# Gated branches summed in PSUM, rotary and router operands kept in PSUM, and the attention sink as one more score of each row

## The chip, the cores and the metric

One core of a Trainium2 chip runs the whole kernel as one program. The metric is the device time of one execution in microseconds (us); before the change it is 1878.28 us, the median of 3 runs (1877.82 to 1882.6). Engines are named as the profile names them: PE (TensorE), DVE (VectorE), ACT (ScalarE), POOL (GpSimd), SP (the queue that issues most DMAs).

## What is computed

One decoder layer, all in float32, for 512 prompt tokens and 8 sequences of 8 new tokens, model width 1024:

```python
z = x @ w_in                      # b_gate, c_gate, h_in, q, k, v, g_conv, g_attn
q, k = rotary(q), rotary(k)       # x * cos + swapped halves of x * (+-sin)
conv_y = short_conv(c_gate * h_in)                 # 3 taps
m = max(max(s), sink); p = exp(s - m)              # window of 128 keys, 8 query heads, 2 KV heads
attn_y = p / (sum(p) + exp(sink - m)) @ v
merged = sigmoid(g_conv) * ((b_gate * conv_y) @ w_conv_out) + sigmoid(g_attn) * (attn_y @ w_attn_out)
h = layer_norm(ALPHA * x + merged @ w_o)
# channel mixer: 8 heads, each the best 16 of 128 x 128 experts by two half keys
y = layer_norm(ALPHA * h + sum_j gate_j * gelu(h . u_j) * v_j)
```

## The kernel before, in words

The 576 tokens are worked in two groups. The first (chunks 0 and SMP: 128 prompt tokens, 64 new tokens and 64 more prompt tokens, 256 columns) has its experts gathered row by row; the second (chunks 1, 2 and 3, 320 tokens) is multiplied with all experts densely. A matmul in float32 is made of three, on a high and a low half of each operand: `split` (L118 to L120) writes the high half on ACT and the low half, the difference, on DVE or POOL. Every weight table of 128x1024 is split so on its way in (`table`, from L136): ACT makes the high half, and POOL or DVE, by the table's number, the low half. POOL's instructions are these subtractions, 2.4 us each for a table, and the issue of the gathers (L511).

Each group passes through these steps: `project_q` and `project_kv` (PSUM banks of pool "mm", of which there are 3), the rotary in `qkv_rope` (from L203), `attention` by chunk and KV head, `conv` by channel tile, `merge_conv`, `merge_attention` (8 tiles dt of 128 model channels, then w_o and the first layer norm), and `scores` with `route`.

In `qkv_rope`, DVE multiplies q and k, which lie in PSUM, by cosine into an SBUF tile t1 (L213) and by sine, with halves swapped, into t2 (L215), and adds the two (L219 for q, L223 for k). In `softmax_parts` (L245 to L265), called once for each chunk and KV head (10 times) and once for the new tokens, DVE takes each row's maximum (L252), its maximum with the sink (L253), the negation (L255) and the sink's difference (L257); ACT takes that one's exponential (L258) and those of the four heads' scores (L261), each with its sum; DVE adds the sink's share (L262). PE then transposes the weights (L301, L345), and DVE and ACT copy them to SBUF (L304, L306).

In `merge_attention`, for each dt PE makes the gate's product (24 matmuls) and the branch's (12 matmuls, in a bank of "mm"). ACT takes the sigmoid `sg` (L671), DVE multiplies it by the branch's product in PSUM (L674), adds the convolution's gated branch `br` (L675), and the sum is split (ACT L119, DVE L120, tiles mhi and mlo). In the PSUM pool "mm" a bank is free for the next product as soon as L674 has read it.

In `route` (L421 to L472), for 4 heads of one chunk at a time, DVE adds the candidates (L429, L432), takes the best 16 (L413 to L417), has ACT take exponentials (L446, L447), normalises (L449 to L451), and finds by integer arithmetic on 64 columns in two passes (L462 to L467) and a comparison with a row of numbers (L469 to L472) which keys they were. From the second group's routing on, that row of numbers lies in columns 384 to 512 of a PSUM tile, `shared[0]`, whose other columns `gate_matrix` (L772 on) fills later with transposes. `route` is called 4 times for the first group and 5 times for the second.

Beside all this runs side work, `experts` (L490): gathers by POOL of rows of the expert tables, one row for each token of the first group at a time, and one DVE instruction of 1024 columns for each (L525, L534). They are put in after weight tables by fixed paces (`side`).

The order of the instructions on each engine is laid out for the whole program by the framework's planner, which follows the data's dependences on a simulated timeline (`TileContext(..., schedule_with_timeline_sim=True)`); the program's order is its priority. On each engine the instructions then run in that fixed order. `late` and `in_order` add orders by hand, on the DMA queue of SP and on PE, and none of them is on a line that changes.

## Time and profile before

| | |
|---|---|
| Median of 3 runs | 1878.28 us |
| The profiled execution | 1882.06 us, its span 1880.3 us |
| PE busy | 1733.5 us (92%) |
| DVE busy | 1507.2 us (80%) |
| POOL busy | 1111.2 us (59%) |
| ACT busy | 782.1 us (42%) |
| Mean granted clock of PE | 0.964 |

Busy time is that in which an engine works on an instruction; for DVE and POOL that includes time in which the instruction has begun and stands. An engine's idle time is put down to the work of another engine that it waited for. The timeline's times are from the start of the span. [...]

### The profile page before, as it was taken

To read this page: it belongs to the slowest core of one execution; us is meant where nothing else is said; L and a number is where in the kernel's file an instruction comes from. 1 tells how busy PE (TensorE), PEld (TensorE's weight loads), DVE (VectorE), ACT (ScalarE), POOL (GpSimd) and SP (SyncE) were. 2 spreads that over 40 slices of the span, in tenths; PEclk is the share of its full clock that TensorE was granted. 3 is DMA by queue.
4 is the path that set the end of the run, shared out by engine and by line. 5 is a ranking of instruction groups with operands and counts; after the bars stand their busy time and mean duration, and the time that the engine had idled before them with its cause. 6 is when DMAs were issued, how large, how long until landed. Compare 5 with 4: busy or idle time off the path is not lost.

```text
span 1880.3 us, 27617 instructions
## 1 busy us (share of the span) xinstructions
PE 1733.5 (92%) x9760; PEld 1573.5 (84%) x9760; DVE 1507.2 (80%) x2632; ACT 782.1 (42%) x1339; POOL 1111.2 (59%) x724
## 2 busy tenths in 40 slices
PE   7999998897989998699979899999999999999985
PEld 7997798887779888699978777787899999998974
DVE  6646689998955699998896677878778888888897
ACT  4554343442333433367785333333333333343322
POOL 4445433466756667688835522223578777778883
PEclk9999999997989999799999899999999999999998
DMA  7445443357757678799947999999989999989973
GB/s 246 156 134 213 130 135 118 113 186 254 277 192 249 232 239 276 248 326 363 338 187 253 330 327 328 345 336 341 322 311 353 335 327 353 350 299 339 326 264 108
DMA packets 190539, 496.50 MB, mean 264 GB/s; under 512 B 17712, under 2 KB 83696, under 8 KB 187312
## 3 DMA queue, kind: packets, MB, share of 16 engines
q1 hardware_dynamic: 135104, 293.39, 45.5%
q0 software_dynamic: 55296, 201.35, 30.1%
q8 instruction: 76, 1.25, 0.3%
q14 instruction: 63, 0.52, 0.1%
HBM read 454.48 MB, written 40.54 MB: 263 GB/s over the span
## 4 chain that ended last, share of the span: by engine, by line
PE 49%; DVE 24%; DMA 10%; issue 7%; POOL 5%; ACT 5%; SPq 1%; DVEq 0%; POOLq 0%; ACTq 0%
PE acc L937 19%; PE ps L123 9%; PE ps L124 8%; PE ps L125 8%; POOL wlo L120 3%; DMA re<-spill 3%; DVE junk L525 3%; PE ps L794 2%; POOL g L511 2%; DVE wlo L120 2%; DMA raw<-in_euT 2%; ACT whi L119 1%; ACT hot L791 1%; DMA g<-in_eu,idx 1%; DVE s L415 1%
## 5 line engine op out<-in xcount | busy, mean ns | idle before, releaser
L120 POOL TENSOR_TENSOR wlo<-raw,whi 128x1024 fp32r<-128x1024 f32 x232 | 580.0, 2503 | 320.6 <-ACT whi L119 287.9
L119 ACT ACTIVATE whi<-raw 128x1024 fp32r<-128x1024 f32 x388 | 409.2, 1056 | 590.0 <-PE ps L124 235.9
L123 PE MATMUL ps<-xhi,whi 128*128 128x384 f32 (+2 forms) x1600 | 531.3, 332 | 34.3 <-ACT sp L860 27.8
L125 PE MATMUL ps<-xhi,wlo 128*128 128x384 f32 (+2 forms) x1600 | 527.4, 330 | 1.6 <-POOL wlo L120 1.6
L124 PE MATMUL ps<-xlo,whi 128*128 128x384 f32 (+2 forms) x1600 | 527.6, 330 | 0.0
L534 DVE SCALAR_TENSOR_TENSOR h<-g,pre,h 128x1024 f32<-128x1024 f32 x192 | 316.2, 1647 | 71.7 <-DMA g<-in_ev,idx 70.4
L511 POOL DMA_INDIRECT g<-in_eu,idx x192 | 206.6, 1076 | 241.3 <-DVE junk L525 186.5
L123 PEld LDWEIGHTS ps<-xhi,whi 128*128 128x128 f32 x1600 | 309.6, 194 | 44.3 <-ACT sp L860 30.3
L511 POOL DMA_INDIRECT g<-in_ev,idx x192 | 255.0, 1328 | 126.5 <-DVE h L534 87.3
L124 PEld LDWEIGHTS ps<-xlo,whi 128*128 128x128 f32 x1600 | 309.3, 193 | 3.6 <-issue 0.9
L125 PEld LDWEIGHTS ps<-xhi,wlo 128*128 128x128 f32 x1600 | 308.6, 193 | 3.0 <-POOL wlo L120 2.1
L937 PE MATMUL acc<-whi,chi 128*128 128x512 f32 x756 | 292.4, 393 | 14.7 <-ACT chi L119 8.4
L937 PE MATMUL acc<-wlo,chi 128*128 128x512 f32 x756 | 299.6, 396 | 5.7 <-POOL wlo L120 5.7
L937 PE MATMUL acc<-whi,clo 128*128 128x512 f32 x756 | 258.1, 394 | 2.1 <-DVE clo L120 2.1
L120 DVE TENSOR_TENSOR wlo<-raw,whi 128x1024 fp32r<-128x1024 f32 x156 | 204.6, 1312 | 49.1 <-ACT whi L119 48.9
L937 PEld LDWEIGHTS acc<-whi,chi 128*128 128x128 f32 x756 | 143.1, 189 | 47.1 <-ACT chi L119 11.7
L937 PEld LDWEIGHTS acc<-wlo,chi 128*128 128x128 f32 x756 | 144.1, 191 | 37.0 <-POOL wlo L120 8.2
L525 DVE SCALAR_TENSOR_TENSOR junk<-g,hp 128x1024 bf16<-128x1024 f32 x104 | 125.7, 1209 | 56.9 <-DMA g<-in_eu,idx 54.8
L937 PEld LDWEIGHTS acc<-whi,clo 128*128 128x128 f32 x756 | 143.6, 190 | 32.8 <-DVE clo L120 2.7
L785 DVE TENSOR_TENSOR hot<-pt,T 128x1024 f32<-128x1024 f32 x96 | 114.0, 1217 | 17.1 <-PE ps L794 12.1
L525 DVE SCALAR_TENSOR_TENSOR junk<-g,h 128x1024 bf16<-128x1024 f32 x88 | 123.7, 1406 | 3.1 <-DMA g<-in_eu,idx 2.8
L794 PE MATMUL ps<-hot 128*128 128x128 f32 x768 | 111.6, 289 | 15.2 <-ACT hot L791 14.0
(252 smaller groups left out, 2205.5 us busy)
## 6 DMA issues: line engine op xcount, KB each, us to landing
raw<-in_euT SPq DMA_DIRECT2D x128, 512.0 KB, 6.1
raw<-in_ev SPq DMA_DIRECT2D x128, 512.0 KB, 5.0
gd<-gb SPq DMA_DIRECT2D x24, 1024.0 KB, 5.2
gm<-gd SPq DMA_DIRECT2D x48, 512.0 KB, 9.7
raw<-in_w_g SPq DMA_DIRECT2D x32, 512.0 KB, 3.4
raw<-in_w_pq SPq DMA_DIRECT2D x32, 512.0 KB, 4.2
raw<-in_w_bch SPq DMA_DIRECT2D x24, 512.0 KB, 3.5
spill<-sp SPq DMA_DIRECT2D x60, 192.0 KB, 4.2
```

The lines of the kernel that those rows point to most:

```text
L119: A.activation(hi, src, AF.Copy)
L120: return (eng or V).tensor_tensor(lo, src, hi.bitcast(F32), op=ALU.subtract)
L123: PE.matmul(ps, L[0], R[0], start=start, stop=False)
L124: PE.matmul(ps, L[0], R[1], start=False, stop=False)
L125: PE.matmul(ps, L[1], R[0], start=False, stop=stop)
L415: V.match_replace(s2, val[:, 0:8], s, -3.0e38)
L511: G.indirect_dma_start(out=rows[i], out_offset=None, in_=I[src], in_offset=bass.IndirectOffsetOnAxis(ap=idx[c][:, s:s + 1], axis=0))
L525: V.scalar_tensor_tensor(junk, g, 1.0, in_psum(c), op0=ALU.mult, op1=ALU.mult, accum_out=p)
L534: V.scalar_tensor_tensor(h_tok[c], g, p, h_tok[c], op0=ALU.mult, op1=ALU.add)
L785: V.tensor_tensor(hot, iota_ps.unsqueeze(1).unsqueeze(1).broadcast_to([128, 2, 4, 128]), T[:, 0:2, n:n + 4].unsqueeze(3).broadcast_to([128 ...
L794: newest[1] = PE.matmul(ps[:, r * 128:(r + 1) * 128], hot[:, 1, r, :], oi, start=True, stop=True).ins
L937: PE.matmul(*args, **kw)
```

## The change

It changes four places.

- `qkv_rope`: the product with cosine is written in place, into the projection's PSUM bank, after the two products with sine have read it; the adds (L219, L223) then read one operand from PSUM.
- `softmax_parts`: the score tile gets one more column for each row and head, into which ACT copies the sink. The row maximum is taken over all columns and written negated in one instruction, the exponentials run over all columns, and their sum holds the sink's share. The maximum with the sink, the negation, the difference, its exponential and the final addition go. Both callers make the tile one column wider; the sink's weight is in a column that no transpose reads.
- `route`: the tiles mk, u1 and gs lie in columns 0 to 132 of `shared[0]` in PSUM, once that tile is there, which is for the second group.
- `merge_attention`: the product with `sg` and the sum with `br` are written in place into the product's PSUM bank, and the split reads it from there.

```diff
--- before.py
+++ after.py
@@ -208,12 +208,12 @@
         out = {}
         for nm, ps, nh in (("q", pq, 8), ("k", pkv, 2)):
             src = ps[:r, :nh * 64].rearrange("p (h d) -> p h d", d=64)
-            t1 = tmp("t", [128, 8, 64], "qT", "r1", 2)[:r, :nh]
+            t1 = src
             t2 = tmp("t", [128, 8, 64], "o", "r2", 2)[:r, :nh]
-            V.tensor_tensor(t1, src, cos.broadcast_to([r, nh, 64]), op=ALU.mult)
             for a, b in ((0, 32), (32, 0)):
                 V.tensor_tensor(t2[:, :, a:a + 32], src[:, :, b:b + 32],
                                 sin[:, a:a + 32].unsqueeze(1).broadcast_to([r, nh, 32]), op=ALU.mult)
+            V.tensor_tensor(t1, src, cos.broadcast_to([r, nh, 64]), op=ALU.mult)
             x = tmp("t", [128, nh * 64], nm + "r", bufs=3)[:r]
             if nm == "q":
                 V.tensor_tensor(x.rearrange("p (g k d) -> p k g d", g=4, k=2),
@@ -243,23 +243,18 @@
         return pt.rearrange("p (g n) -> p g n", g=4)[:, :, :r], pk[:, :r]
 
     def softmax_parts(s, sink, name):
-        r, n = s.shape[:2]
+
+        r, n, m = s.shape
 
         def small(tag):
             return tmp("t", [128, n], tag, name + tag, 2)[:r]
 
-        mx = small("mx")
-        V.tensor_reduce(mx, s, axis=AX.X, op=ALU.max)
-        V.tensor_tensor(mx, mx, sink, op=ALU.max)
+        A.activation(s[:, :, m - 1:m], sink.unsqueeze(2), AF.Copy)
         ngm = small("ngm")
-        V.tensor_scalar(ngm, mx, -1.0, None, op0=ALU.mult)
-        es = small("es")
-        V.tensor_tensor(es, sink, mx, op=ALU.subtract)
-        A.activation(es, es, AF.Exp)
+        V.tensor_reduce(ngm, s, axis=AX.X, op=ALU.max, negate=True)
         den = small("den")
         for i in range(n):
             A.activation(s[:, i, :], s[:, i, :], AF.Exp, bias=ngm[:, i:i + 1], accum_out=den[:, i:i + 1])
-        V.tensor_tensor(den, den, es, op=ALU.add)
         rd = small("rd")
         V.reciprocal(rd, den)
         return rd
@@ -284,7 +279,8 @@
         mask = mask_p[:r, k0 + 128 - q0:k0 + 128 - q0 + nk]
         o = tmp("t", [128, 4, 2, 64], "o", bufs=2)[:r]
         for kv in range(2):
-            st = tmp("t", [128, 1024], "t4", bufs=3)[:r].rearrange("p (g k) -> p g k", g=4)[:, :, :nk]
+            sa = tmp("t", [128, 1028], "t4", bufs=3)[:r].rearrange("p (g k) -> p g k", g=4)[:, :, :nk + 1]
+            st = sa[:, :, :nk]
             for gp2 in range(2):
                 ps = bank("at")[:r]
                 for j in range(2):
@@ -293,7 +289,7 @@
                 V.scalar_tensor_tensor(st[:, gp2 * 2:gp2 * 2 + 2, :],
                                        ps.rearrange("p (j k) -> p j k", j=2)[:, :, :nk], SCALE,
                                        mask.unsqueeze(1).broadcast_to([r, 2, nk]), op0=ALU.mult, op1=ALU.add)
-            rd = softmax_parts(st, sink_p[:r, kv * 4:kv * 4 + 4], "p")
+            rd = softmax_parts(sa, sink_p[:r, kv * 4:kv * 4 + 4], "p")
             pT = tmp("t", [128, 1024], "t4", bufs=3).rearrange("p (b g n) -> p b g n", b=2, g=4)[:, :, :, :r]
             for b, (at, n, _, _) in enumerate(blocks):
                 ps = bank("at")
@@ -324,7 +320,8 @@
         qf = qT.rearrange("p b g t -> p (b g t)")
         mask_s = tmp("t", [128, 2, 192], "mask_s")
         late(mask_s, I["mask_s"])
-        st = tmp("t", [128, 1024], "t4", bufs=3)[:, :768].rearrange("p (k b s) -> p k b s", k=2, b=2)
+        sa = tmp("t", [128, 1028], "t4", bufs=3)[:, :772].rearrange("p (k b s) -> p k b s", k=2, b=2)
+        st = sa[:, :, :, :192]
         for kv in range(2):
             r = slice(kv * 64, kv * 64 + 64)
             ps = bank("at")
@@ -337,7 +334,7 @@
                               start=True, stop=True, tile_position=(kv * 64, bl * 32))
             V.scalar_tensor_tensor(st[:, kv], ps[:, :384].rearrange("p (b s) -> p b s", b=2), SCALE, mask_s,
                                    op0=ALU.mult, op1=ALU.add)
-        sf = st.rearrange("p k b s -> p (k b) s")
+        sf = sa.rearrange("p k b s -> p (k b) s")
         rd = softmax_parts(sf, sink_s.rearrange("p k b -> p (k b)"), "s")
         pc = bank("at")
         pn = bank("at")
@@ -416,7 +413,7 @@
         V.max(val[:, 8:16], s2)
         V.max_index(pos[:, 8:16], val[:, 8:16], s2)
 
-    numbers = [iota]
+    numbers, scratch = [iota], []
 
     def route(val, pos, sel, hs):
 
@@ -434,6 +431,10 @@
                         v4[:, :, 1, 0:4].unsqueeze(2).broadcast_to([r, 4, 12, 4]), op=ALU.add)
 
         def f128(tag, dt=F32):
+            if scratch and tag in ("mk", "u1"):
+                at = 64 * ("mk", "u1").index(tag)
+                t = scratch[0][:r, at:at + 64]
+                return t if dt == F32 else t.bitcast(dt)
             return tmp("k", [128, 64], tag, dt=dt)[:r]
 
         bv = f128("bv")
@@ -445,7 +446,7 @@
         ge = f128("ge").rearrange("p (h k) -> p h k", h=4)
         V.tensor_tensor(ge, b3, b3[:, :, 0:1].broadcast_to([r, 4, 16]), op=ALU.subtract)
         A.activation(ge, ge, AF.Exp)
-        gs = tmp("k", [128, 4], "gs")[:r]
+        gs = scratch[0][:r, 128:132] if scratch else tmp("k", [128, 4], "gs")[:r]
         V.tensor_reduce(gs, ge, axis=AX.X, op=ALU.add)
         V.reciprocal(gs, gs)
         V.tensor_tensor(gt.rearrange("p (h k) -> p h k", h=4), ge,
@@ -671,9 +672,10 @@
             A.activation(sg, product(s, weight(s, I["w_g"][dt, 1]), s.xT, 8, "u"), AF.Sigmoid)
             if dt % 2 == 0:
                 wt = weight(s, I["w_ca"][dt // 2])
-            V.tensor_tensor(sg, sg, product(s, wt, s.at, 4, "mm", dt % 2 * 4), op=ALU.mult)
-            V.tensor_tensor(sg, sg, s.br[:, dt, :], op=ALU.add)
-            split(mg[0][:, dt, :], mg[1][:, dt, :], sg)
+            ps = product(s, wt, s.at, 4, "mm", dt % 2 * 4)
+            V.tensor_tensor(ps, sg, ps, op=ALU.mult)
+            V.tensor_tensor(ps, ps, s.br[:, dt, :], op=ALU.add)
+            split(mg[0][:, dt, :], mg[1][:, dt, :], ps)
         s.rs.close()
         if s.w == 0:
             pools["h"] = s.rs.enter_context(pool("h", "left"))
@@ -844,6 +846,7 @@
     shared = [pools["at"].tile([128, 512], F32, tag="at", name="pt")]
     A.activation(shared[0][:, 384:512], iota128, AF.Copy)
     numbers[0] = shared[0][:, 384:512]
+    scratch.append(shared[0])
     pools["hp"] = ks.enter_context(psum("hp", 1))
     pools["f"] = ctx.enter_context(pool("f", "right"))
     pools["b"] = bs.enter_context(pool("b", "right"))
```

## Rows read from the trace of the kernel before

**Rows 1.** Busy time by 40 us windows: PE, PEld, DVE, ACT, POOL, granted clock, DMA.
```profile
120.00:160.00 40.00, 40.00 (x328) 39.43 (x327) 22.49 (x30) 18.31 (x31) 17.77 (x9) 1.00 0.56 198
...
200.00:240.00 40.00, 36.64 (x263) 33.92 (x262) 21.16 (x49) 15.19 (x24) 15.97 (x7) 0.96 0.39 121
...
320.00:360.00 40.00, 33.13 (x218) 31.27 (x217) 40.00 (x131) 13.73 (x29) 17.43 (x7) 0.91 0.33 111
...
760.00:800.00 40.00, 31.90 (x156) 31.59 (x157) 39.95 (x98) 13.96 (x20) 26.61 (x17) 0.80 0.75 240
```

**Rows 2.** Waits of PE from 0 to 600 us: total us, times, longest.
```profile
PE ps L301 <- ACT t L261: 18.2, 8, 9.8
```

**Rows 3.** Waits of all engines from 640 to 800 us.
```profile
ACT ge L447 <- DVE ge L446: 35.3, 5, 11.6
...
PE ps L123 <- ACT sp L860: 26.7, 6, 10.1
```

**Rows 4.** Lines L674, L675, L219 and L255 by themselves: shortest, median, longest ns.
```profile
L674 DVE TENSOR_TENSOR sg<-sg,ps x16: 420/447/489, 132.3 to 482.4; 128x256 f32<-128x256 f32 x8, 128x320 f32<-128x320 f32 x8
...
L675 DVE TENSOR_TENSOR sg<-sg,br x16: 414/1834/2702, 132.7 to 482.9; 128x256 f32<-128x256 f32 x8, 128x320 f32<-128x320 f32 x8
...
L219 DVE TENSOR_TENSOR qr<-r,r x5: 670/877/2203, 21.7 to 229.7; 128x512 f32<-128x512 f32 x4, 64x512 f32<-64x512 f32 x1
...
L255 DVE TENSOR_SCALAR pngm<-pmx x10: 141/170/2109, 44.8 to 428.7; 128x4 f32<-128x4 f32 x8, 64x4 f32<-64x4 f32 x2
```

**Rows 5.** Timeline of DVE and POOL at 724 us: start, duration, instruction.
```profile
724.10 2.92 DVE L466 TENSOR_TENSOR rk<-rk,mk 128x64 f32<-128x64 f32 x1
...
724.54 2.38 POOL L120 TENSOR_TENSOR wlo<-raw,whi 128x1024 fp32r<-128x1024 f32 x1
...
726.94 0.18 DVE L463 TENSOR_SCALAR u<-bp 128x64 uint32<-128x64 uint32 x1
```

**Rows 6.** Groups of DVE instructions by line and shape, 640 to 830 us.
```profile
L466 DVE TENSOR_TENSOR rk<-rk,mk 128x64 f32<-128x64 f32 x10 | 11.2, 1115 | 0.0
...
L467 DVE TENSOR_TENSOR rk<-rk,u 128x64 f32<-128x64 f32 x10 | 5.9, 594 | 0.0
...
L462 DVE TENSOR_SCALAR u<-bp 128x64 uint32<-128x64 uint32 x10 | 4.3, 432 | 0.0
...
L451 DVE TENSOR_TENSOR gt<-ge,gs 128x64 f32<-128x64 f32 x4 | 2.8, 710 | 0.0
```

**Rows 7.** Timeline at 417 to 430 us, around the last softmax: DVE, ACT, PE.
```profile
417.58 0.93 DVE L252 TENSOR_REDUCE pmx<-t 64x4 f32<-64x768 f32 x1
...
420.74 1.28 ACT L261 ACT_TABLE_LOAD   x1
...
428.73 0.15 DVE L255 TENSOR_SCALAR pngm<-pmx 64x4 f32<-64x4 f32 x1
...
428.92 0.45 ACT L261 ACTIVATE t<-t,pngm 64x192 f32<-64x192 f32 x1 [6.90 <-DVE pngm L255]
...
431.44 0.42 DVE L306 COPY t<-ps 64x256 f32<-64x256 f32 x1
...
429.52 1.88 PE L301 MATMUL ps<-ident,t 64*128 64x64 f32 x8 [9.79 <-ACT t L261]
```

**Rows 8.** Timeline at 334 to 338 us, around another softmax: DVE, ACT.
```profile
334.04 1.19 DVE L252 TENSOR_REDUCE pmx<-t 128x4 f32<-128x1024 f32 x1
...
337.83 0.51 ACT L261 ACTIVATE t<-t,pngm 128x256 f32<-128x256 f32 x1 [8.09 <-DVE pngm L255]
```

**Rows 9.** Busy time by two windows behind that last softmax, columns of rows 1.
```profile
430.00:443.00 13.00, 11.02 (x46) 8.77 (x47) 9.90 (x21) 3.69 (x9) 8.87 (x7) 0.50 0.76 247
...
443.00:480.00 37.00, 35.24 (x227) 34.79 (x226) 33.47 (x40) 12.59 (x19) 26.89 (x16) 0.95 0.78 273
```

**Rows 10.** Timeline of DVE at 445 to 455 us: first merge tile of the second group.
```profile
444.96 0.49 DVE L674 TENSOR_TENSOR sg<-sg,ps 128x320 f32<-128x320 f32 x1
...
455.08 0.48 DVE L120 TENSOR_TENSOR mlo<-sg,mhi 128x320 fp32r<-128x320 f32 x1
```

## The prediction

> **What bounds the kernel now.** I read the busy time by 40 us windows first, then the waits of PE and of ACT, then the timeline at the longest of those waits, and last the groups of DVE instructions in the stretch where DVE never rests. The windows [rows 1] say that no one engine bounds all of it. In the merge of the first token group (120 to 160 us) PE is busy for all of its 40 us while DVE works 22 us: nothing that is saved on DVE there can show. While the rotary of the second group runs (200 to 240 us) PE is still at 36.6 of 40. From 280 us on the picture turns over: at 320 to 360 us DVE is busy for 40.00 of 40 us and PE for 33, and at 760 to 800 us DVE for 39.95 and PE for 31.9, at a granted clock of 0.80. Those two stretches, attention of the second group with routing of the first, and routing of the second group, are where DVE sets the time.
>
> The waits say how DVE's lateness reaches PE. Up to 600 us PE's transposes of the softmax weights (L301) wait 18.2 us for ACT's exponentials, one of these waits lasting 9.8 us [rows 2]. From 640 to 800 us ACT stands for 35.3 us before the exponential of the router (L447) until DVE has made its operand, and PE stands for 26.7 us because the Gelu that frees its bank (L860) is queued behind that on ACT [rows 3].
>
> Why is DVE slow there? Two lines of the merge tell it. L674 multiplies a tile in SBUF by one in PSUM and takes 420 to 489 ns in all 16 cases; L675 adds two SBUF tiles of the same shapes and takes 414 ns at best, 1834 in the median and 2702 at worst [rows 4]. At 724 us a product of 64 columns (L466, two SBUF operands) takes 2.92 us, and ends as POOL's subtraction (724.54 plus 2.38) ends; the next DVE instruction then runs in 0.18 us [rows 5]. So an instruction of DVE with two SBUF operands waits until POOL's instruction in flight is done, and one with a PSUM operand does not. A DVE instruction with one SBUF operand and an SBUF result can wait too: L462, 64 columns, has a mean of 432 ns [rows 6] where L463, the same operation and shape, takes 0.18 us [rows 5].
>
> **The change, part by part.**
>
> *Router (mk, u1, gs in PSUM).* Only the second token group has the scratch tile: 5 of 9 calls, all between 640 and 810 us. Per call two passes of L462, L465, L466 and L467, and L451, leave the kind that waits for POOL. Unhindered they take about 0.2 us (0.18 for the scalar forms). From [rows 6] what goes is at most: L467 10 times (0.594 - 0.21) = 3.8 us, L462 10 times (0.432 - 0.18) = 2.5 us, L451 4 times (0.710 - 0.21) = 2.0 us, and L466 10 times (1.115 - 0.21) = 9.1 us. L466 I count at nothing: behind it on DVE comes L463 [rows 5], which writes u2 from SBUF to SBUF and is left as it is, so it will stand and wait for the same POOL instruction. Of the other 8.3 us I count 7.5, since some of it will fall on the next instruction with two SBUF operands. DVE is full here and PE waits at its end, so all 7.5 us are on the path. Ends: 0 if every wait moves on, 17.4 if none does.
>
> *Softmax.* Eleven calls lose four small DVE instructions each (maximum with the sink, negation, difference, final addition) and swap an exponential of four values on ACT for a copy of four values. The negation alone takes 0.14 us at best and 2.11 at worst [rows 4]. What matters is the chain: the exponentials can follow the row maximum directly. Before the last softmax the maximum ends at 418.51, ACT has its table at 422.02, but the negation is not done before 428.88, as it and the maximum with the sink are queued behind other DVE work; PE's transposes begin at 429.52 after 9.79 us of idling [rows 7]. By the order of need they could begin 428.92 - 422.02 = 6.9 us sooner; but the copy of the transposes (L306, 431.44) stands on DVE behind the same work and would be late next. If its place stays, only the small instructions go, some 0.4 us. I take half, 3.5. At 338 us the maximum ends at 335.23 and the exponentials start at 337.83 [rows 8]: ACT had idled 8.09 us, so 2.4 us are free to go. The seven other waits of [rows 2], PE's share of this one among them, sum to 18.2 - 9.8 = 8.4 us; of the rest I count 1.2. [...] Softmax together: 3.5 + 2.4 + 1.2 + 1.0 = 8.1 us, ends 1 and 16.
>
> The sink's copy is a new wait, of DVE for ACT: the row maximum now reads that column too. Behind the maximum on DVE stands all else of that stretch. The copy can go as soon as the tile is free, before the scores are there, so I take 0; the upper end stands among the rivals.
>
> *Merge.* 16 times L675 and the subtraction behind it get a PSUM operand. At the median L675 loses 1.4 us, 22 us of DVE in all. Eight of the 16 lie under a full PE (0 gained); in the other eight PE works 35.2 of 37 us [rows 9], and DVE's expert gather instructions, which keep both operands in SBUF, stand next in line for the same POOL instruction. I count 0.4 of the 1.8 us that PE idles there; ends 0 and 1.8. A price of it: the product's bank is held from L674 until the subtraction. For the first tile of the second group that is 444.96 to 455.56, 10.6 us [rows 10]. There are three banks; a tile takes 36 matmuls, 36/227 of 37 us = 5.9 us [rows 9], so the bank is wanted again three tiles on less its own 12 matmuls, 17.6 - 2.0 = 15.6 us after the product. 5 us to spare, so 0.
>
> *Rotary.* t1 stays in the projection's bank and the add (L219, 670 ns at best, 877 in the median) no longer waits for POOL. The bank is let go one instruction of 0.7 us later, five times. PE is busy 36.6 of 40 us meanwhile [rows 1]: 0, ends -2 and +2.
>
> *Writing into PSUM from DVE* has no row. The nearest are L674, whose PSUM operand costs 6 ns over L675 at its shortest [rows 4], which I take: 0.6 us over some 100 instructions, in all the small ones. The far end: if reading and writing one bank doubled them, the 55 of the router would cost 0.2 us more each, 11 us, and the gain of the router would be gone.
>
> [...]
>
> **Sum.** 7.5 + 8.1 + 0.4 + 0 = 16.0 us. What is saved ahead of 800 us moves everything after it as it stands. The profiled execution took 1882.1 us (a span of 1880.3 and 1.8 around it), 3.8 above the median of the runs, 1878.3. Off the one, 1866; off the median, which I forecast, 1878.3 - 16.0 = 1862.3.
>
> **The rivals.** *The waits only move.* Each wait for POOL falls on the next instruction with SBUF operands, L463 and the gather first, and the order of DVE stays. Then 2.4 us at 338 us, 0.4 at 429 and 1 us elsewhere are left: 1874 to 1878. For it speaks L463 behind L466 [rows 5]; against it that L451 and L467 are followed by no such neighbour in the sums of rows 6.
>
> *All of it shows.* Router 17.4, softmax 16, merge 1.8, less the 0.6: 1844. It needs the copy L306 and L463 to be placed anew; the order of each engine is laid out by a planner for the whole program, so it can be.
>
> *The sink's copy holds DVE up.* ACT works in order and had stood 8.09 and 6.90 us before exponentials [rows 7, 8]. If the copy is queued behind an instruction of ACT that itself waits for DVE, the row maximum and all behind it stand still. With a wait of 4 us, half of these, at six softmaxes of the second group, DVE loses 24 us where it is full, and softmax's gain is gone: 1878.3 - 7.9 + 24 = 1894. It decides from about 1.3 us per softmax (7.9/6) on. Against it: four columns, no operand but the sink.
>
> **How the numbers follow.** A measurement of this kernel can tell 0.3%, 5.6 us, from no change. Forecast 0.48, all of it 0.18 (together faster, 0.66); only moved 0.20 (no change); held up 0.14 (slower). The likeliest is 1862. The range goes from all of it, 1844, up to 1881, past the cases in which the waits only move, and leaves out the slower one and a little at the bottom.
>
> **What would show it.** Right: L675 and the subtractions at 0.42 to 0.49 us each; L467, L451 and L462 of the second group near 0.2 us in every case, with L463 now up to 2 us; PE's wait for the last softmax at some 6 us; PE's waits for L860 shorter by a third. Wrong: L252 idling for ACT, PE waiting for the merge's subtraction, or L466 and L467 longer than 0.3 us while POOL is idle.

## The result, and the profile after

The changed kernel takes 1851.6 us (median of 4 runs, 1848.17 to 1932.96), the kernel before 1878.05 on the same chip (4 runs, 1877.21 to 1882.6): a ratio of 0.9849, 95% interval 0.9831 to 0.9868. One of the four runs was slow (1932.96 us, at a granted clock of 0.834) and is left out of the ratio; the other three have their median at 1850.18 us, which is the time of the changed kernel wherever others are compared with it below. By the median of all four the change takes 26.5 us off, in the range (1844 to 1881) and of the sign that was forecast, but 10 us more than the sum of 16.0. The profiled execution took 1850.18 us, its span 1848.4.

First the page's busy times of the kernel after. DVE has lost 42.5 us (1507.2 before), PE 9.6, and PE's mean granted clock, of which 1.00 is the full speed, is 0.972 for 0.964.

```profile
PE 1723.9 (93%) x9760; PEld 1566.4 (85%) x9760; DVE 1464.7 (79%) x2588; ACT 781.4 (42%) x1337; POOL 1109.6 (60%) x724
```

The windows of [rows 1] in the kernel after; the last is that of the second group's routing, taken 16 us earlier, since that routing now starts 14.7 us sooner (632.3 for 647.0).

```profile
120.00:160.00 40.00, 40.00 (x333) 39.81 (x332) 17.46 (x29) 18.79 (x31) 20.38 (x9) 1.00 0.58 206
200.00:240.00 40.00, 37.24 (x261) 34.48 (x260) 19.12 (x52) 15.17 (x26) 15.90 (x7) 0.96 0.45 139
320.00:360.00 40.00, 38.17 (x249) 36.30 (x250) 40.00 (x151) 18.54 (x38) 14.03 (x6) 0.91 0.32 106
744.00:784.00 40.00, 31.34 (x162) 30.38 (x162) 39.79 (x86) 13.77 (x20) 28.56 (x19) 0.87 0.81 276
```

DVE is still full in the last two, so it bounds those stages as before; but in the third PE does 38.2 us of work beside it where it did 33.1.

PE's waits from 0 to 600 us, after (in [rows 2] the exponentials cost 18.2 us, 8 times, at worst 9.8), and then the waits of all engines from 616 to 784 us, which answer to [rows 3].

```profile
PE ps L722 <- DVE h L200: 14.8, 3, 8.7
PE ps L123 <- ACT whi L119: 9.0, 2, 6.8
PE ps L123 <- DVE mlo L120: 3.6, 1, 3.6
PE ps L134 <- DVE t L302: 3.4, 2, 1.8
...
PE ps L297 <- ACT t L257: 2.7, 2, 2.1
```

```profile
ACT ge L448 <- DVE ge L447: 21.7, 5, 7.8
...
PE ps L123 <- ACT sp L863: 13.4, 4, 6.3
```

The waits for the exponentials are 2.7 us, 15.5 less; those behind the router 13.4, half of the 26.7. Two things stand on the other side: a wait of 3.6 us until the first group's last mlo is made, and the layer norm's (L722), 14.8 us where it was 12.3.

The three edited lines by themselves, shortest, median and longest ns (L676 is the product, L677 the sum, L254 the maximum; [rows 4]):

```profile
L676 DVE TENSOR_TENSOR ps<-sg,ps x16: 428/454/493, 129.2 to 462.9; 128x256 f32<-128x256 f32 x8, 128x320 f32<-128x320 f32 x8
...
L677 DVE TENSOR_TENSOR ps<-ps,br x16: 418/458/500, 129.6 to 463.4; 128x256 f32<-128x256 f32 x8, 128x320 f32<-128x320 f32 x8
...
L254 DVE TENSOR_REDUCE sngm<-t x1: 956/956/956, 70.8 to 70.8; 128x4 f32<-128x772 f32 x1
its engine sat idle before it (us, times) until:
  ACT t L252: 0.3, 1
```

The sum has no case left above 500 ns. Of eleven maxima one has DVE waiting for the sink's copy, 0.3 us.

The groups of DVE instructions of the second group's routing, 600 to 800 us, after; below them two lines of the view of [rows 6], of the kernel before, that the prediction did not use. L464 is the old L463, L472 the old L471, L463, L466 to L468 and L452 the old L462, L465 to L467 and L451 of [rows 6].

```profile
L472 DVE TENSOR_TENSOR oh<-oh,pf 128x1024 bf16<-128x1024 bf16 x10 | 11.7, 1172 | 0.1
...
L464 DVE TENSOR_SCALAR u<-bp 128x64 uint32<-128x64 uint32 x10 | 7.9, 790 | 0.0
...
L463 DVE TENSOR_SCALAR pt<-bp 128x64 uint32<-128x64 uint32 x10 | 2.1, 215 | 0.0
L466 DVE SCALAR_TENSOR_TENSOR rk<-u,pt 128x64 f32<-128x64 uint32 x10 | 2.1, 209 | 0.1
L468 DVE TENSOR_TENSOR rk<-rk,pt 128x64 f32<-128x64 f32 x10 | 2.0, 204 | 0.0
L467 DVE TENSOR_TENSOR rk<-rk,pt 128x64 f32<-128x64 f32 x10 | 2.0, 203 | 0.1
...
L452 DVE TENSOR_TENSOR gt<-ge,pt 128x64 f32<-128x64 f32 x4 | 0.8, 200 | 0.0
```

```profile
L471 DVE TENSOR_TENSOR oh<-oh,pf 128x1024 bf16<-128x1024 bf16 x10 | 18.4, 1837 | 0.0
...
L463 DVE TENSOR_SCALAR u<-bp 128x64 uint32<-128x64 uint32 x10 | 1.9, 193 | 0.0
```

What was given a PSUM operand or result takes 200 to 215 ns in the mean. The u2 line behind it went from 1.9 to 7.9 us, as forecast in kind; the one-hot product fell from 18.4 to 11.7, which nobody had counted.

Where the 26.5 us come from can be read from three points of each trace: the first transposes of the gate matrix, the first accumulating matmul (the start of what I call the dense stage) and the end of the span.

| kernel | first transposes | first accumulation | end | dense stage |
|---|---|---|---|---|
| before | 806.2 | 1062.4 | 1880.3 | 817.9 |
| after | 778.1 | 1033.3 | 1848.4 | 815.1 |

The traces are 31.9 us apart, more than the medians, as the profiled run of the kernel before was 4 us above its median. Of these 31.9 us 28.1 are there at the transposes, at 778 us, and 29.1 at the dense stage. When ACT copies the second group's first scores the lead (how much sooner than in the kernel before) is 15.8 us (557.9 and 542.1); at PE's own matmuls for these scores it is 12.5 to 14.4. So attention and merge gave some 13 to 16 us, the routing some 12 to 15, and the rest of the program little. That reading was one trace of each kernel; the experiments ask whether the parts really are worth this.

### The profile page after: what moved, and what is told of

Same layout as the page of the kernel before. It is cut to its first block, busy times and chain, and to the rows that moved or that the text cites. A ratio compares the mean times of both kernels' runs of the same rounds, so it can differ in the third digit from the quotient of the medians.

```text
span 1848.4 us, 27569 instructions
## 1 busy us (share of the span) xinstructions
PE 1723.9 (93%) x9760; PEld 1566.4 (85%) x9760; DVE 1464.7 (79%) x2588; ACT 781.4 (42%) x1337; POOL 1109.6 (60%) x724
## 4 chain that ended last, share of the span: by engine, by line
PE 40%; DVE 23%; DMA 14%; issue 9%; POOL 8%; ACT 4%; SPq 1%; DVEq 0%; POOLq 0%; ACTq 0%
PE acc L940 15%; PE ps L123 7%; PE ps L124 7%; PE ps L125 7%; DMA g<-in_ev,idx 5%; POOL wlo L120 4%; POOL g L512 4%; DVE junk L526 3%; PE ps L796 3%; DMA re<-spill 2%; DVE wlo L120 2%; DMA raw<-in_ev 2%; DMA raw<-in_w_o 1%; ACT whi L119 1%; ACT hot L793 1%
## 5 line engine op out<-in xcount | busy, mean ns | idle before, releaser
L123 PE MATMUL ps<-xhi,whi 128*128 128x384 f32 (+2 forms) x1600 | 529.9, 331 | 21.6 <-ACT sp L863 13.4
L535 DVE SCALAR_TENSOR_TENSOR h<-g,pre,h 128x1024 f32<-128x1024 f32 x192 | 309.8, 1614 | 68.3 <-DMA g<-in_ev,idx 66.8
L526 DVE SCALAR_TENSOR_TENSOR junk<-g,h 128x1024 bf16<-128x1024 f32 x88 | 130.9, 1488 | 3.3 <-DMA g<-in_eu,idx 3.0
L796 PE MATMUL ps<-hot 128*128 128x128 f32 x768 | 113.4, 290 | 14.5 <-ACT hot L793 13.4
L787 DVE TENSOR_TENSOR hot<-pt,T 128x1024 f32<-128x1024 f32 x96 | 113.9, 1218 | 15.8 <-PE ps L796 12.7
```

The lines of the kernel that those rows point to most:

```text
L123: PE.matmul(ps, L[0], R[0], start=start, stop=False)
L526: V.scalar_tensor_tensor(junk, g, 1.0, in_psum(c), op0=ALU.mult, op1=ALU.mult, accum_out=p)
L535: V.scalar_tensor_tensor(h_tok[c], g, p, h_tok[c], op0=ALU.mult, op1=ALU.add)
L787: V.tensor_tensor(hot, iota_ps.unsqueeze(1).unsqueeze(1).broadcast_to([128, 2, 4, 128]), T[:, 0:2, n:n + 4].unsqueeze(3).broadcast_to([128 ...
L796: newest[1] = PE.matmul(ps[:, r * 128:(r + 1) * 128], hot[:, 1, r, :], oi, start=True, stop=True).ins
```

## The experiments

**One part alone.** Each of the first four kernels is the kernel before with one part of the change; a line or two of each edit is shown, and `...` stands for lines left out.

```diff
 softmax alone
-        V.tensor_reduce(mx, s, axis=AX.X, op=ALU.max)
...
+        A.activation(s[:, :, m - 1:m], sink.unsqueeze(2), AF.Copy)
...
+        V.tensor_reduce(ngm, s, axis=AX.X, op=ALU.max, negate=True)
```

> Theory A (each part takes away its own waits where DVE or PE stands): the softmax part alone brings some 12 us, to about 1866, the PE wait for the last softmax of the second group (9.8 us before) falls to 2 or 3 us, and the maximum never stands for the sink's copy. Theory B (the planner's new order brings the gain, and the parts don't add up): any value from 1860 to 1885, and the four parts alone sum to less than 15 or more than 40 us where the whole brings 26.5. Rival C (the sink's copy holds DVE up): 1880 or more, with DVE idle for ACT before the maximum.

```diff
 router alone
+            if scratch and tag in ("mk", "u1"):
...
-        gs = tmp("k", [128, 4], "gs")[:r]
+        gs = scratch[0][:r, 128:132] if scratch else tmp("k", [128, 4], "gs")[:r]
```

> Theory A: the router part alone brings some 12 us, to about 1866; the time from 0 to 560 us is as before within 2 us, the gate matrix starts 10 to 13 us earlier than at 806 us, and u2 (the scalar operation that is left in SBUF) takes over some 6 us of waits for POOL. Theory B: the time up to 640 us, where nothing is changed, moves by several us too. Rival (the waits only move): 1875 or more, with the DVE waits in the stretch the same in sum.

```diff
 merge alone
-            V.tensor_tensor(sg, sg, s.br[:, dt, :], op=ALU.add)
-            split(mg[0][:, dt, :], mg[1][:, dt, :], sg)
+            V.tensor_tensor(ps, ps, s.br[:, dt, :], op=ALU.add)
+            split(mg[0][:, dt, :], mg[1][:, dt, :], ps)
```

> Theory A: within 3 us of before (1875 to 1881): the first merge lies under a full PE, and in the second DVE's gathers take over the waits for POOL; the two tiles' lines run at 0.42 to 0.49 us. Theory B: anything from 1865 to 1890. The bank that is held longer would show as PE waiting for the low half (mlo) before a branch product.

```diff
 rotary alone
-            t1 = tmp("t", [128, 8, 64], "qT", "r1", 2)[:r, :nh]
+            t1 = src
...
```

> Theory A: within 3 us of before (1875 to 1881), as PE is busy 36.6 of 40 us meanwhile. Theory B: anything from 1865 to 1890, from the order alone, since the rotary tiles also leave the buffers of qT and o.

**All but one.** The next four are the changed kernel with one of these edits taken back, of which one line is shown.

```diff
 without merge: the merge edit above in reverse
+            V.tensor_tensor(sg, sg, s.br[:, dt, :], op=ALU.add)
```

> Theory A2 (softmax and merge work as a pair: softmax alone brought the first product of the second merge 14.7 us forward and lost 13 of it over the next tiles, where L675 and the gathers stand for POOL): without the merge part the gate matrix starts some 17 us earlier than before instead of 28, the time is about 1862, and the second merge takes longer than in the whole change. Theory B (order alone): no such pairing; anywhere from 1850 to 1875, and the second merge takes as long as in the whole change.

```diff
 without softmax: the softmax edit in reverse
+        V.tensor_tensor(mx, mx, sink, op=ALU.max)
```

> Theory A2: the wait of 9 to 10 us for the last softmax is back, the merge part has nothing to pass on, and what is left is the router's: gate matrix some 12 to 14 us earlier than before, time about 1866 to 1870. Theory B: from 1850 to 1880, with the wait for the last softmax gone or smaller.

```diff
 without router: the router edit in reverse
+        gs = tmp("k", [128, 4], "gs")[:r]
```

> Theory A2: scores of the second group some 14 to 16 us earlier than before, as in the whole change, and that same lead at the gate matrix, PE waiting some 27 us for L860 as before; time about 1863 to 1866. Theory B: the lead at 540 us is not that of the whole change.

```diff
 without rotary: the rotary edit in reverse
+            t1 = tmp("t", [128, 8, 64], "qT", "r1", 2)[:r, :nh]
```

> Theory A2: rotary alone cost 3 us up to the gate matrix; without it the whole is 0 to 4 us faster still, 1848 to 1852. Theory B (order alone): the time may be up to 15 us longer, as other changes get another order.

Measured, each beside runs of the kernel before on its chip (1879.71 us for the first four, 1878.05 for the others):

| kernel | us (lowest to highest) | ratio, 95% interval | first transposes | dense stage |
|---|---|---|---|---|
| softmax alone | 1878.18 (1869.91–1885.08) | 0.9994 [0.9969, 1.0018] | 800.9 | 816.4 |
| router alone | 1874.0 (1869.13–1885.7) | 0.9977 [0.9951, 1.0003] | 792.1 | 822.2 |
| merge alone | 1877.88 (1873.03–1882.73) | 0.9991 [0.9967, 1.0015] | 805.5 | 814.3 |
| rotary alone | 1891.74 (1885.49–1908.02) | 1.0061 [1.0029, 1.0093] | 808.9 | 827.0 |
| without merge | 1857.49 (1854.3–1860.01) | 0.9893 [0.9867, 0.992] | 785.1 | 812.5 |
| without softmax | 1881.65 (1868.91–1891.01) | 1.0018 [0.9992, 1.0043] | 791.8 | 828.1 |
| without router | 1877.78 (1869.08–1884.28) | 0.9994 [0.9968, 1.002] | 793.7 | 828.5 |
| without rotary | 1867.14 (1863.85–1869.81) | 0.9941 [0.9919, 0.9963] | 784.8 | 827.6 |

By their medians the parts alone give +3.0 us together where the whole gives -26.5, and rotary costs 12 us alone but is worth 17 inside the change (1867.1 less 1850.2). Prices of parts can't be like that. The column on the right says where most of it lies: the dense stage, on whose lines nothing was edited, takes 812 to 818 us in the kernels before, after, softmax alone, merge alone and without merge, and 822 to 829 in the others. The leads at the first transposes are plainer: -14.1 for the router alone, -5.3 for softmax, -0.7 for merge, +2.7 for rotary. But they don't add up either: together 17.4 us alone, and 43 us by the four parts taken back (15.6 for the router, 13.7 softmax, 7.0 merge, 6.7 rotary), where the whole has 28.1. The parts work on one another ahead of the dense stage too.

PE and DVE by windows say where in that stage: the first 320 us of it in the kernel after (from 1033) and without router (from 1049).

```profile
1033.00:1353.00 320.00, 311.46 (x1394) 260.46 (x1395) 252.25 (x351) 111.77 (x149) 114.61 (x90) 0.99 0.97 336
```

```profile
1049.00:1369.00 320.00, 305.31 (x1332) 253.72 (x1333) 246.49 (x344) 108.84 (x144) 105.27 (x85) 0.97 0.94 324
```

62 matmuls fewer in the same time, at a DMA share of 0.94 for 0.97: so the DMA engines are not fuller there. The SP queue of the kernel without router, and ACT beside it:

```profile
1077.04 5.09 SPq L897 DMA_DIRECT2D gm<-gd  x3
1082.23 2.76 SPq L138 DMA_DIRECT2D raw<-in_ev  x1
1085.09 0.47 SPq L901 DMA_DIRECT2D re<-spill  x1
1085.65 0.39 SPq L138 DMA_DIRECT2D raw<-in_ev  x1
1086.13 1.17 SPq L901 DMA_DIRECT2D re<-spill  x2
1087.44 10.86 SPq L138 DMA_DIRECT2D raw<-in_ev  x3
1099.58 5.54 SPq L901 DMA_DIRECT2D re<-spill  x3
```

```profile
1092.41 1.06 ACT L119 ACTIVATE whi<-raw 128x1024 fp32r<-128x1024 f32 x1 [6.25 <-DMA raw<-in_ev]
1095.02 1.06 ACT L119 ACTIVATE whi<-raw 128x1024 fp32r<-128x1024 f32 x1 [1.55 <-DMA raw<-in_ev]
1096.42 0.99 ACT L119 ACTIVATE chi<-re 128x384 fp32r<-128x384 f32 x2 [0.35 <-DVE re L905]
```

Behind the three reads of the gate matrix come loads of tables (L138) and reads of row blocks (L901) in clumps, three loads ahead of three reads. On ACT the splits of two loaded tables stand ahead of both splits chi (the high half of a row block, which PE multiplies with), and the first of them stands 6.25 us for its load; PE waits 3.8 us for chi, and there are three such waits up to 1350 us. The clump of three loads and three reads stands three times in the SP order of each of the five kernels with a stage of 822 us or more; of the other five, softmax alone has it once, and the rest never. Up to 1350 us each clump has a wait of PE for chi of 2.6 to 4.6 us, 8 to 10 us behind it (in rotary alone two of the three have); the kernels without a clump have none above 1.8 us there, but for the first accumulation. The order is laid by the planner, which lays the whole program anew for any edit: no line of this stage differs.

**Loads and reads in turn.** So the order was forced, with one edit:

```diff
-        newest[0] = S.dma_start(raw, src).ins
...
+            with tc.issue_after(behind):
+                newest[0] = S.dma_start(raw, src).ins
...
-            S.dma_start(ge, spill[t])
+            spilled[t] = S.dma_start(ge, spill[t]).ins
...
+                   PACE_V[t >= NS], spilled.get(t - 8))
```

(`behind` is the read of row block t - 8, where there is one), in the whole change, and in the change without its router part:

> The whole change, and in the dense stage (from the first accumulating matmul to the end) each load of a raw tile of expert_v is put on SP's queue behind the read of the spilled row block eight before it, so that loads and reads go in turn and no three loads stand ahead of a read. Two theories of why that stage took 812 to 818 us in five of the ten kernels measured so far (before 818.0, after 815.1) and 822 to 829 in the others. Theory A, SP's order: three loads ahead of a read make the read late, DVE's product with it, ACT's split chi, and PE waits 3.5 to 4.7 us, three times. Then this kernel's stage is 810 to 816 us, it has no wait of PE for chi above 2.5 us, and the time is 1846 to 1853 us. Theory B, the transfers' share: 16 DMA engines are at 0.9 to 1.0 there, so a lead that arrives early is given back whatever the order: the stage stays at 815 +- 2 us and the time at 1850 to 1853 us. This run alone does not tell them apart; it is the other side of the next one.

> The change without its router part (1877.8 us, stage 828.5 us), with the loads and reads put in turn as in the run above. Theory A: the stage falls by 10 to 15 us to 812 to 818 us, PE's three waits of 3.5 to 4.3 us for chi go, and the time is 1863 to 1868 us; the distance to the run above is then what the router part is worth, 12 to 16 us, about its lead at the gate matrix when it was alone (14.0 us). Theory B: the stage stays at 825 to 829 us and the time at 1875 to 1880 us, within 0.2% of the kernel before.

and, after these were known, in the change without its rotary part:

> The change without its rotary part (1867.1 us, dense stage 827.6 us, three of PE's waits for chi of 3.0 to 4.0 us), with the loads and reads of the dense stage put in turn. Theory A, SP's order sets the stage: it falls to 816 to 822 us and the time to 1854 to 1861 us; the distance to the whole change in turn (1847.1 us) is then what the rotary part is worth inside the change, 7 to 13 us, as its lead at the first scores of the second group (5.1 us without it, 15.8 with it) says, and rotary alone cost 13 us only by the order that came with it. Theory B: the stage stays at 825 to 829 us and the time at 1864 to 1868 us. A third way: with this order laid anew the merge loses no lead either, the time is within 3 us of the whole change in turn, and the rotary part is worth nothing, as was forecast.

| kernel, in turn | us (lowest to highest) | ratio, 95% interval | first transposes | dense stage | without the edit |
|---|---|---|---|---|---|
| whole change | 1847.14 (1840.85–1855.0) | 0.984 [0.9795, 0.9884] | 782.3 | 818.1 | 1850.2, 815.1 |
| without router | 1860.22 (1852.31–1873.92) | 0.9909 [0.9878, 0.994] | 793.1 | 820.2 | 1877.78, 828.5 |
| without rotary | 1845.99 (1844.64–1852.99) | 0.9841 [0.9817, 0.9865] | 780.5 | 815.9 | 1867.14, 827.6 |

Theory A holds where it matters: with no edit but that of the order, the kernel without router is 17.6 us faster and the one without rotary 21.2, beyond their intervals, and their dense stages lose 8 and 12 us; the whole change, whose order was good already, stays within what its runs scatter. Theory B, by which order makes no difference, falls. Three details of A were off. The stages came out at 820.2 without router and not 812 to 818 (one wait of 3.9 us for chi is left), and at 818.1 for the whole change and not 810 to 816. Only half of the gain without router lies in that stage: the other half lies between the transposes and the first accumulation, 247.7 us for 255.8, and so it does in the whole change, 246.4 for 255.2; the first accumulation no longer waits 5.3 us for its split table. And the late thing was not the row block alone but the split chi standing behind the splits of the loads. The edit constrains SP only, and the planner then lays ACT and DVE anew too, so which of the three queues does the harm is not told apart; that the order laid does it, and not the lines of the part, is. The edit moved earlier stages as well, where it has no line: the copy of the first scores came 3.9 us later in the whole change (546.0), 2.5 later without router (544.5), and 9.3 sooner without rotary (543.5 for 552.8). So two kernels in turn still differ in layout ahead of the dense stage. For rotary the third way came true: without it the kernel is at 1846.0 us, with it at 1847.1. It is worth nothing that these runs can tell. The 12 us that it cost alone are for 9.1 the dense stage (827.0 for 817.9); of what it seemed to be worth inside, 12 us went with the dense stage's order and some 9 with the layout ahead of that stage.

**u2 moved too.** The changed kernel left L464's wait. Here u2 goes to PSUM as well, and u1, mk and the last sum are worked so that no operation of the two passes has SBUF on all sides (p0 and p1 are 64 columns each of the scratch bank; lines are left out at `...`):

```diff
+                u2 = p0.bitcast(U32)
+                V.tensor_single_scalar(u2, bp, s2[0], op=s2[1])
...
+                V.scalar_tensor_tensor(p1, u2, off, u1, op0=ALU.add, op1=ALU.subtract)
+                V.tensor_tensor(p1, p1, mk, op=ALU.mult)
+                V.tensor_tensor(rk, p1, u1, op=ALU.add)
```

> The whole change with the loads and reads in turn, and the router's second pass operand u2 moved too: each operation of the two passes of the second token group has one operand or its result in PSUM (a shift or mask more per pass, some 0.2 us each, ten calls, +2 us of DVE). Theory A of the router, the wait belongs to the form of the instruction: the 6.1 us that L464 waited for POOL vanish, the sum of waits for POOL in 624 to 784 us falls from 27 to some 21 us, the first transposes of the gate matrix come 3 to 6 us earlier than in the whole change in turn, and so does the end. Rival, the wait only moves on: the next instruction with two SBUF operands (the differences of route, the one-hot products) takes it, the first transposes come at the same time or 2 us later.

It takes 1838.94 us (1836.88 to 1842.58), a ratio of 0.9799, 0.9768 to 0.9831: the fastest kernel of the study, 39 us below the kernel before. Groups of DVE instructions from 628 to 788 us, first of the whole change in turn, then with u2 moved:

```profile
L468 DVE TENSOR_SCALAR u<-bp 128x64 uint32<-128x64 uint32 x10 | 8.3, 826 | 0.0
...
L462 DVE CAST pf<-pos 128x128 bf16<-128x128 uint32 x5 | 6.2, 1238 | 0.0
```

```profile
L492 DVE TENSOR_TENSOR oh<-oh,pf 128x1024 bf16<-128x1024 bf16 x10 | 11.3, 1133 | 0.2
...
L478 DVE SCALAR_TENSOR_TENSOR pt<-pt,u 128x64 f32<-128x64 uint32 x10 | 2.2, 217 | 0.0
...
L464 DVE CAST pf<-pos 128x128 bf16<-128x128 uint32 x5 | 1.5, 304 | 0.0
```

No operation of the passes is above 220 ns in the mean; the cast pf falls from 6.2 to 1.5 us too, and only the one-hot product takes a little back (9.9 us before, 11.3). Over all its lines the second group's routing takes 69.0 us of DVE for 79.1. So the wait belongs to the form, and does not simply move on. The routing ends 6.0 us sooner (781.7 for 787.7), but the first transposes came only 0.7 us sooner (781.6), where 3 to 6 were expected: PE is busy 168.1 us from 620 to 800, 4.8 more than in the whole change in turn, so the lead first went into matmuls that stood earlier in PE's order. By the first accumulation it is 9.9 us (1018.8 for 1028.7). The intervals of these two kernels still overlap, so the 8.2 us between their medians are not clear of scatter; that of the change (0.9831 to 0.9868) only touches this one's, and all four runs lie below the fastest of the change (1848.17).

## Why the prediction was right, and where it was too small

**Router: 7.5 forecast, some 13 measured** (1860.2 less 1847.1, both in turn; 10.8 us at the first transposes and 14.2 at the ends of the two traces). The two sets of runs spread over 22 and 14 us, so by an estimate from that spread the 13 is good to some 9 us. The three lines that were counted gave 3.9 (old L467), 2.2 (L462) and 2.0 us (L451), 8.1 against 8.3; old L465, which the prediction names but gives no term, gave 1.2. The step that was mis-sized is "L466 I count at nothing": it lost 9.2 us and its neighbour u2 took over 6.0, not all. The one-hot product, on which no line was edited, lost 6.7 us more. It has two SBUF operands, and with fewer stops for POOL ahead of it it met fewer of POOL's subtractions; that last reason is argued, the number is shown. The routing's other lines took some 4 us back. Over all its lines the second group's routing takes 77.8 us of DVE for 93.1, 15.3 less; between the two kernels in turn it is 13.3 less (79.1 for 92.4), and 13 show.

**Softmax: 8.1 forecast, more measured.** The step was "If its place stays, only the small instructions go ... I take half, 3.5". Its place did not stay: the last row maximum starts at 388.36 us instead of 417.58, and PE's wait of 9.8 us is gone, not shortened (the longest is now 2.1, where some 6 was forecast). That goes with the softmax part and no other: in the nine kernels that have it the last maximum starts at 388 to 399 us and PE's longest wait for the exponentials is 2.1 to 3.5 us, in the five without it 415 to 422 and 8.3 to 9.8. The sum of 8.1 has a term of 1.0, the author's estimate for the granted clock behind that wait, which no run shows as a time by itself; what the runs show in its place is the clock of one 60 us window, 380 to 440 us, before and after:

```profile
380.00:440.00 60.00, 48.21 (x294) 42.22 (x294) 57.16 (x125) 23.12 (x43) 39.91 (x22) 0.84 0.63 211
```

```profile
380.00:440.00 60.00, 56.64 (x374) 51.81 (x373) 59.61 (x100) 22.92 (x38) 45.29 (x28) 1.00 0.79 257
```

PE is busy 8.4 us longer and does 80 matmuls more, at a granted clock of 1.00 for 0.84. Without the softmax part the window is as before (47.82 us, 287 matmuls, 0.84). The part alone has a lead of 11.6 us at the first sum of the second merge (436.1 for 447.7) and of only 5.3 at the transposes; why it shrinks is not shown, as the kernel without rotary, which has the merge part too, loses it the same way (10.6, and 5.1 at the first scores). Inside the change the first scores come 15.8 us sooner than before, and without the softmax part not at all (0.8 later); at the transposes 13.7 us hang on it (791.8 and 778.1). What the merge and the layout add to that cannot be cut apart further: without merge the lead at the first scores is 11.4 us. The change without softmax was not run with the order held, so this part's price in time stays open.

**Merge: 0.4 forecast; 0 alone, 7.3 inside** (1857.5 less 1850.2). The durations are as forecast, 454 and 458 ns. The step that failed is "5 us to spare, so 0", the price of the bank that is held longer: it was worked out for the first tile of the second group, and the wait came at the last tile of the first, 3.6 us of PE until the subtraction mlo had read the bank. PE waiting for that subtraction was one of the prediction's own signs of being wrong. DVE of the kernel after, from 159 us:

```profile
159.99 2.32 DVE L120 TENSOR_TENSOR xlo<-g,xhi 128x960 fp32r<-128x960 f32 x1 [0.26 <-ACT xhi L119]
162.24 0.42 DVE L677 TENSOR_TENSOR ps<-ps,br 128x256 f32<-128x256 f32 x1
162.57 2.55 DVE L120 TENSOR_TENSOR xlo<-g,xhi 128x640 fp32r<-128x640 f32 x1
165.05 3.37 DVE L120 TENSOR_TENSOR wlo<-raw,whi 128x1024 fp32r<-128x1024 f32 x1
168.34 0.41 DVE L120 TENSOR_TENSOR mlo<-ps,mhi 128x256 fp32r<-128x256 f32 x1
```

L677 itself takes 0.42 us where it took 2.48 in the kernel before (at 162.82), but three splits of the second group's tables and inputs stand around it, and the subtraction, the last in the row, lets the bank go only at 168.75. PE's next product there, first in the changed kernel, then without the merge part, with the subtraction of the latter:

```profile
168.90 0.76 PE L123 MATMUL ps<-whi,mhi 128*128 128x512 f32 x1 [3.64 <-DVE mlo L120]
```

```profile
163.90 0.50 PE L123 MATMUL ps<-whi,mhi 128*128 128x512 f32 x1 [0.98 <-ACT whi L119]
```

```profile
168.62 0.41 DVE L120 TENSOR_TENSOR mlo<-sg,mhi 128x256 fp32r<-128x256 f32 x1
```

This product reads high halves alone, and without the merge part it starts 4.7 us ahead of a subtraction that comes as late. So it is the bank that PE waits for, and not the low half: all nine kernels with the merge part have this wait (3.2 to 3.6 us at the longest), and none of the five others. Inside the change the merge's share is one pair of layouts, not a clean price.

**Rotary: 0 forecast, 0 found** (1847.1 with, 1846.0 without), once the order was held.

**"What is saved ahead of 800 us moves everything after it as it stands"**: true of this change (28.1 us at the transposes, 31.9 at the end), but by its layout's luck. Four kernels of the eight took 9 to 11 us more than the kernel before for a stage that no line of theirs touched, and a fifth 4.

**The rivals.** "The waits only move" fell with the groups; of what L466 lost, two thirds went on to u2. "The sink's copy holds DVE up" fell with DVE's one wait of 0.3 us: the copy runs at 378.95, 9 us ahead of the last maximum. "All of it shows" (1844) was nearer than the forecast; of what it needed, that things be placed anew, the softmax was, and u2 was not.

**PSUM as a target** of DVE's writes, the term with the widest ends (0.6 to 11 us), costs little. The merge's product, written in place into its bank (L676), takes 428 ns at its shortest and 454 in the median where L674, into SBUF, took 420 and 447. The shift L463 takes 215 ns in the median into PSUM (the second group) and 183 into SBUF (the first), 32 ns more. A PSUM source costs nothing that can be seen: old L466 took 196 ns at its shortest and 216 in the median with both operands in SBUF, the new L467, which reads mk from PSUM, 193 and 198. (The 55 of the router that the prediction counts are 60 in the program, of which 40 read PSUM.)

## What to carry to other kernels

Ask of each DVE instruction beside a busy POOL whether it has two SBUF operands, or one and an SBUF result (here L464, into SBUF, took up to 2.87 us beside POOL's subtractions, and L463, into PSUM, 0.23 at most), and give one side to a PSUM bank that is free anyway, after a look at who wants that bank next; count the instructions behind it too, as a wait that goes can take others along. Where a planner lays the whole program anew for each edit, a part alone or a part taken back measures the part and a new layout: compare stages of the traces that the edit does not touch, and hold the order of such a stage by hand before prices are subtracted; what lies ahead of that stage can still be laid out anew. A lead gained early is only worth what the later stages' queues let through.

## What had not been expected of the hardware

That a DVE operation with one SBUF operand and an SBUF result can wait was in the prediction; that it can stand as long as one with two was not (2.87 us at its longest, the old L466 3.05). L464 (64 columns) takes 184 ns in the median, but three times it took 1.43, 2.23 and 2.87 us, each ending within 0.07 us of the end of a subtraction of POOL (the last 770.73 and 770.67). The same operation into PSUM (L463) never takes more than 229 ns: at 665.05 us it ran in 0.22 inside the subtraction (664.67 to 667.07) for which the L464 behind it, at 665.70, then stood 1.43. In these rows a PSUM result took the instruction out of the wait, and so did a PSUM operand for L467, which at 665.56 us ran in 0.22 inside the same subtraction; why an instruction with SBUF on all sides waits there no row here shows.

The clock: PE had a granted clock of 1.00 from 400 to 420 us, worked 0.5 us in the next ten, and had 0.50 behind that. There products of 128x320 followed each other every 0.267 us, and every 0.147 at 1.00 (from 440 and from 410 us). By an estimate from these two the 11.0 us that it then worked [rows 9] are 6.1 at 1.00, so the stall of 9.8 us cost half as much again; with the stall gone the whole window had 1.00.
